# Windowed attention scores: tiles of 64 queries of two heads in place of 128 queries of one head

## The chip, the cores and the metric

The kernel runs on one core of a Trainium2 chip, as one program. Its time is the device time of one execution in microseconds; lower is better. The time before is 1047.88 us, the median of three runs (1046.16 to 1048.37).

## The reference, cut to what matters

One encoder block over T = 1040 positions (16 meta tokens and 1024 positions of the sequence), with D = 1024. From one input projection come a retention branch (4 heads) and an attention branch (8 heads in 2 groups of keys, head dimension 128), each with a SiLU gate and a projection; sigmoid gates merge them, and an output projection, a norm and a residual end the block. The change lies in the attention branch:

```python
ok = (jnp.abs(qpos[:, :, None] - kp) <= WINDOW) & (kp >= CHUNK) & (kp < Lp)   # WINDOW = CHUNK = 128
s_band = jnp.einsum("bnqgrd,bnkgd->bngrqk", qb, kb) * scale
s_band = jnp.where(ok[None, :, None, None], s_band, NEG_INF)
s_meta = jnp.einsum("bnqgrd,bmgd->bngrqm", qb, km) * scale
s = jnp.concatenate([s_band, s_meta], axis=-1)
m = jnp.maximum(jnp.max(s, axis=-1, keepdims=True), sink_l)
p = jnp.exp(s - m)
p = p / (jnp.sum(p, axis=-1, keepdims=True) + jnp.exp(sink_l - m))
o = (jnp.einsum("bngrqk,bnkgd->bnqgrd", p[..., :3 * CHUNK], vb)
     + jnp.einsum("bngrqm,bmgd->bnqgrd", p[..., 3 * CHUNK:], vm))
```

A query sees the keys at most 128 positions away on either side, the 16 meta keys, and a sink logit that adds to the sum alone. A block of 128 queries so sees parts of three blocks of keys: 384 keys, and 16 meta keys.

## The kernel before

Every fp32 matrix product is made of three fp32r products: both operands are split into a rounded high part and the rest, and `mm3` (L74) issues high x high (L76), low x high (L77) and high x low (L78). Splits are a copy on ACT or POOL for the high part and a subtraction on DVE (`dve_lo`, L92) for the low part.

The program is written in the order in which engines are to be fed; a scheduler turns it into a list per engine, and `follow` (L81) ties instructions behind others. The stages are: projections and retention, head by head; then attention, into which projections of later heads and products of the next stage are woven as filling; then gates (z), the two branch projections (r and a) and the output projection (o).

Attention (L1379) runs over `chunks`: four pairs of heads `hp` (two heads `e_` of one group of keys), and for each eight blocks `n` of 128 queries. A chunk passes three stages:

- `stage1` (L1384): six score matmuls into two banks of PSUM, 128 queries of one head by a span of key columns each. The keys of a group lie in `kh` and `kl` with the 16 meta keys repeated in each 272 columns, so one span of 400 columns holds the three blocks and the meta keys (272 columns for block 0 and block 7). One DVE instruction (L1416) adds the mask, scales, keeps the minimum against the negated sink and writes `raw`; ACT takes the exponential with its sum (L1419), the sink's column with it; DVE takes the reciprocal `den` (L1422); POOL scales both heads' weights `p` in place (L1429) and copies the meta columns twice into `pm2` (L1437, recorded as L89). In the last two chunks ACT does POOL's part (L1426, L1435).
- `stage2` (L1440): TensorE transposes the weights, 128 columns at a time: L1446 for two blocks of keys, L1451 for the third, L1452 for the meta columns; ACT and DVE split them.
- `stage3` (L1476): TensorE multiplies with the values (`po`), ACT copies the result to `oa` (L1487), and it goes out by DMA.

In program order a round is: stage1 of chunk k+1, stage2 of chunk k, filling (`fill`, by `FILL`, mostly 5 to 9 steps of three matmuls of 512 columns), stage3 of chunk k-1. The scores of a chunk are so made one round before its weights are transposed. Queries are rotated by `rope_late` (L180, two accumulating DMAs on POOL's queue) and split by `split_q` (L661: ACT L667, DVE L92) per head and half of the sequence; `BEGUN` (L1539) says at which step of the filling.

Of the kernel before, what the change touches and what calls it, by code (L numbers as in the profile page):

```python
# [7 lines left out]
F32 = mybir.dt.float32  # L8
# [31 lines left out]
def block_kernel(ctx: ExitStack, tc: tile.TileContext, x0, xT, x, meta, w_in, w_rb, w_ab, w_out, post_w,  # L40
# [52 lines left out]


    vec = keep.tile([P, 2 * KT], F32, name="vec")
    nsink = edge.tile([P, 24], F32, name="nsink")[:, 0:8]
# [169 lines left out]
    with tc.tile_pool(name="setup", bufs=1, reuse_waits="tile") as st:  # L266
# [81 lines left out]
            qk0_mm(k)  # L348
        decay_columns()
        with follow(low):  # L350
            nc.vector.tensor_scalar(nsink, head[:, 29:37], -1.0, None, op0=ALU.mult)
# [308 lines left out]

    def split_q(hp, e_, i):  # L661

        o = aq[hp][e_, i]
        h, l = (aw.tile([P, 512], R, tag=f"aq{t}", bufs=4, name=f"aq{t}{hp}_{i}{e_}") for t in "hl")
        if not aqs:
            aw.tile([P, 48], F32, name="space_aq")
        nc.scalar.copy(h, o)  # L667
        dve_lo(l, o, h)
        aqs[hp, e_, i] = h, l


    def fetch_aq(hp):
# [703 lines left out]
    for t in pm:  # L1376
        nc.vector.memset(t.bitcast(F32), 0.0)

    def attention():  # L1379
        oa = [None]  # L1380
        raw = [aw.tile([P, 401], F32, tag=f"raw{e_}", bufs=1, name=f"raw{e_}") for e_ in range(2)]
        st1, st2 = {}, {}

        def stage1(hp, n):  # L1384
            g = hp // 2
            kh, kl = (t.rearrange("p a b -> p (a b)") for t in kT[g])
            if n == 0:
                start, wid, mo, blocks, moff = 0, 272, 144, [(0, 0), (1, 128)], 256
            else:
                start = 272 * ((n - 1) // 2) + 128 * ((n - 1) % 2)  # L1390
                mo = 0
                wid = 272 if n == 7 else 400
                if n % 2:
                    blocks, moff = [(n - 1, 0), (n, 128), (n + 1, 272)], 256
                else:
                    blocks, moff = [(n - 1, 0), (n, 144), (n + 1, 272)], 128
                if n == 7:
                    blocks = blocks[:2]
            i, o0 = n // 4, P * (n % 4)
            nm_ = ap.tile([P, 2], F32, tag="nm", bufs=3, name=f"nm{hp}_{n}")  # L1400
            den = ap.tile([P, 2], F32, tag="den", bufs=3, name=f"den{hp}_{n}")
            pt = []
            pp = ap.tile([P, 2, 401], F32, tag="p", bufs=2, name=f"p{hp}_{n}")
            for e_ in range(2):
                hd = 2 * hp + e_
                if (hp, e_, i) not in aqs:
                    split_q(hp, e_, i)
                a_, b_ = (t[:, o0:o0 + P] for t in aqs[hp, e_, i])
                s = p2(f"ps{hd}_{n}")
                mm3(s[:, 0:wid], a_, b_, kh[:, start:start + wid], kl[:, start:start + wid], True, True)  # L1410
                if n == 0:
                    if hp:
                        raw[e_] = aw.tile([P, 401], F32, tag=f"raw{e_}", bufs=1, name=f"raw{hd}")
                    nc.vector.tensor_copy(raw[e_][:, 0:1], nsink[:, hd:hd + 1])
                p = pp[:, e_]
                nc.vector.tensor_tensor_reduce(raw[e_][:, 1:1 + wid], s[:, 0:wid], mask[0][:, mo:mo + wid], -SCALE,  # L1416
                                               nsink[:, hd:hd + 1], ALU.add, ALU.min, nm_[:, e_:e_ + 1])

                last["exp"] = nc.scalar.activation(p[:, 0:1 + wid], raw[e_][:, 0:1 + wid], AF.Exp, scale=-1.0,  # L1419
                                                   bias=nm_[:, e_:e_ + 1], accum_out=den[:, e_:e_ + 1]).ins  # L1420
                pt.append(p[:, 1:401])
            last["sum"] = nc.vector.reciprocal(den, den).ins  # L1422
            softmax.append(last["sum"])
            for e_ in range(2):
                if hp == 3 and n > 5:
                    softmax.append(nc.scalar.activation(pt[e_][:, 0:wid], pt[e_][:, 0:wid], AF.Copy,  # L1426
                                                        scale=den[:, e_:e_ + 1]).ins)
                    continue
                nc.gpsimd.tensor_scalar(pt[e_][:, 0:wid], pt[e_][:, 0:wid], den[:, e_:e_ + 1], 1.0, op0=ALU.mult,  # L1429
                                        op1=ALU.mult)  # L1430
# [3 lines left out]
            if hp == 3 and n > 5:  # L1434
                softmax.append(nc.scalar.copy(both, w_).ins)  # L1435
            else:
                pool_hi(both, w_)  # L1437
            st1[hp, n] = (pt, blocks, both.rearrange("p a b c -> p (a b c)"))

        def stage2(hp, n):  # L1440
            pt, blocks, both = st1.pop((hp, n))
            t1 = p1(f"pt1_{hp}_{n}")
            for j in range(2):
                for e_ in range(2):
                    o = blocks[j][1]
                    nc.tensor.transpose(t1[:, 256 * j + P * e_:256 * j + P * e_ + P], pt[e_][:, o:o + P], ident)  # L1446
            t2 = p1(f"pt2_{hp}_{n}")
            if len(blocks) > 2:
                for e_ in range(2):
                    o = blocks[2][1]  # L1450
                    nc.tensor.transpose(t2[:, 256 + P * e_:256 + P * e_ + P], pt[e_][:, o:o + P], ident)  # L1451
# [24 lines left out]
        def stage3(hp, n):  # L1476
# [121 lines left out]
def _constants():  # L1598
    import numpy as np

    f = np.float32
    half = 64
    inv = (f(10000.0) ** (-np.arange(half, dtype=f) * f(2.0) / f(128.0))).astype(f)
    pos = np.arange(T, dtype=f)
    ang = pos[:, None] * inv[None, :]
    c, s = np.cos(ang).T.astype(f), np.sin(ang).T.astype(f)
    rope = np.stack([np.concatenate([c, c], 0), np.concatenate([s, -s], 0)])
    j = np.arange(P)
    prev = np.where(j[None, :] >= j[:, None], 0.0, -1e30)
    nxt = np.where(j[None, :] <= j[:, None], 0.0, -1e30)  # L1610
    z = np.zeros((P, 144))
    rel = j[None, :] - j[:, None]
    idx = np.stack([127 - j, j, j + 1, 128 - j, np.maximum(15 - j, 0)], 1)
    tab = np.concatenate([prev, z, nxt, z[:, :16], np.eye(P), np.maximum(rel, 0), np.maximum(-rel, 0)], 1)
    return np.ascontiguousarray(rope), np.ascontiguousarray(tab.astype(f)), idx.astype(f)


def arrange(inputs):
# [5 lines left out]
    def units(w, order):  # L1624
# [10 lines left out]
    xT = con(np.concatenate([meta, x], 0).T.reshape(KT, P, T))  # L1635
    dec = np.concatenate([i["ret_decay_fwd"][0], i["ret_decay_bwd"][0]])
    small = [i["pre_norm_w"][0].reshape(KT, P).T, i["ret_norm_w"][0].reshape(KT, P).T, np.tile(dec, (P, 1)), idx,
             np.tile(i["attn_sink"][0], (P, 1)), np.zeros((P, 3), np.float32)]
    nat = list(range(8))
    return {  # L1640
        "x0": con(np.concatenate(small + [xT[0]], 1)),
# [31 lines left out]
```

## Time and profile before

| | |
|---|---|
| median of three runs | 1047.88 us (1046.16 to 1048.37) |
| the profiled execution | 1045.47 us |
| its span, first to last instruction | 1043.4 us |
| granted TensorE clock | 0.998 |
| DVE, ACT, POOL busy | 80%, 48%, 22% of the span |
| attention, about 332 to 546 us | 214 us |

Times of the trace are counted from the span's start. A group's row ends with busy time in all, mean of one, and the idle time of its engine just before it with what ended it. A record of a matmul is as long as its way through the array, and consecutive ones overlap; their starts tell their price. PEld is the loading of a stationary operand, which lies beside other matmuls.

### The profile page before, as it was taken

The numbers are of one execution on the slowest core, as the hardware profiler recorded it, in microseconds if no ns is written. First come the engines' busy times: TensorE is split into PE (matmuls) and PEld (weight loads), VectorE is DVE, ScalarE is ACT, GpSimd is POOL, SyncE is SP. The second block draws the span as 40 slices with busy tenths as digits, with TensorE's granted clock in tenths as the row PEclk, the third lists the DMA queues.
The fourth block names the chain that finished last, engine by engine and source line by source line (L and its number), as shares of the span: only waits on it lengthen the run. The fifth ranks groups of instructions, "written<-read, shape, count | busy, mean of one in ns | idle before, by whom it ended". The sixth has DMA issues, their size and how long they took to land. (4 is left out here: it accounts for less than half of the span.)

```text
span 1043.4 us, 17240 instructions
## 1 busy us (share of the span) xinstructions
PE 1029.0 (99%) x5880; PEld 901.9 (86%) x5880; DVE 838.1 (80%) x1788; ACT 505.7 (48%) x1127; POOL 228.2 (22%) x338
## 2 busy tenths in 40 slices
PE   9999999999999999999999999999999999999997
PEld 8998999989989888988888888777888788788886
DVE  7786758768875787878769988998899899778665
ACT  5541432423524566665677554555557446334443
POOL 3444244243342333443310000000000000111042
PEclk9999999999999999999999999999999999999999
DMA  9434223243231466676549679899935746799563
GB/s 353 165 88 88 64 46 85 78 88 103 78 91 62 102 182 188 172 184 164 162 165 340 191 255 322 308 325 346 392 109 178 248 159 231 223 236 317 134 122 80
DMA packets 98838, 188.43 MB, mean 181 GB/s; under 512 B 13024, under 2 KB 37632, under 8 KB 98192
## 3 DMA queue, kind: packets, MB, share of 16 engines
q1 hardware_dynamic: 81200, 162.89, 46.5%
q0 software_dynamic: 10176, 14.73, 9.4%
q10 hardware_dynamic: 7376, 9.73, 2.7%
q8 instruction: 46, 0.75, 0.3%
q14 instruction: 40, 0.33, 0.1%
HBM read 124.32 MB, written 57.68 MB: 174 GB/s over the span
## 5 line engine op out<-in xcount | busy, mean ns | idle before, releaser
L1287 POOL DMA_DIRECT2D mx_d<-c1a x4 | 3.6, 889 | 395.7 <-DVE c1a L1278 377.5
L77 PE MATMUL bz<-big,llz 128*128 128x512 f32 x192 | 74.9, 390 | 0.2 <-DVE llz L92 0.2
L76 PE MATMUL bz<-big,lhz 128*128 128x512 f32 x192 | 74.0, 390 | 0.5 <-ACT lhz L974 0.5
L78 PE MATMUL bz<-big,lhz 128*128 128x512 f32 x192 | 74.2, 389 | 0.0
L76 PE MATMUL pv<-wh,big 128*128 128x256 f32 x256 | 72.8, 284 | 0.0
L77 PE MATMUL pv<-wh,big 128*128 128x256 f32 x256 | 72.7, 284 | 0.0
L78 PE MATMUL pv<-wl,big 128*128 128x256 f32 x256 | 72.7, 284 | 0.0
L77 PE MATMUL bz<-T,llz 128*128 128x512 f32 x176 | 68.6, 390 | 0.7 <-DVE llz L92 0.7
L76 PE MATMUL bz<-T,lhz 128*128 128x512 f32 x176 | 68.2, 390 | 0.5 <-DVE u2z L1064 0.5
L78 PE MATMUL bz<-T,lhz 128*128 128x512 f32 x176 | 68.5, 389 | 0.0
L1419 ACT ACTIVATE p<-raw,nm 128x401 f32<-128x401 f32 (+1 forms) x64 | 38.3, 600 | 34.7 <-DVE nm L1416 33.3
L1429 POOL TENSOR_SCALAR p<-p,den 128x400 f32<-128x400 f32 (+1 forms) x60 | 37.8, 687 | 67.1 <-DVE den L1422 65.2
L76 PE MATMUL paq<-big,wh 128*128 128x512 f32 x128 | 51.5, 402 | 0.0
L77 PE MATMUL paq<-big,wl 128*128 128x512 f32 x128 | 50.2, 392 | 0.1
L78 PE MATMUL paq<-big,wh 128*128 128x512 f32 x128 | 50.2, 393 | 0.0
L76 PEld LDWEIGHTS pv<-wh,big 128*128 128x128 f32 x256 | 48.3, 189 | 0.4
L77 PEld LDWEIGHTS pv<-wh,big 128*128 128x128 f32 x256 | 48.3, 189 | 0.4
L78 PEld LDWEIGHTS pv<-wl,big 128*128 128x128 f32 x256 | 48.2, 188 | 0.3
L76 PEld LDWEIGHTS bz<-big,lhz 128*128 128x128 f32 x192 | 36.1, 188 | 8.5 <-ACT lhz L974 1.1
L92 DVE TENSOR_TENSOR wl<-wr,wh 128x1024 fp32r<-128x1024 f32 x28 | 35.1, 1258 | 10.0 <-POOL wh L89 6.7
L77 PEld LDWEIGHTS bz<-big,llz 128*128 128x128 f32 x192 | 36.0, 188 | 7.9 <-DVE llz L92 0.5
L78 PEld LDWEIGHTS bz<-big,lhz 128*128 128x128 f32 x192 | 36.0, 188 | 7.5
(616 smaller groups left out, 3594.7 us busy)
## 6 DMA issues: line engine op xcount, KB each, us to landing
wrz<-in_w_in_dram SPq DMA_DIRECT2D x32, 512.0 KB, 6.1
wr<-in_w_in_dram SPq DMA_DIRECT2D x29, 512.0 KB, 4.0
we<-in_w_in_dram SPq DMA_DIRECT2D x16, 512.0 KB, 4.2
tg<-tg_d SPq DMA_DIRECT2D x32, 256.0 KB, 4.9
e<-e ACTq DMA_DIRECT2D x20, 256.0 KB, 2.6
e<-e SPq DMA_DIRECT2D x20, 256.0 KB, 4.9
xn<-in_x_dram SPq DMA_DIRECT2D x8, 512.0 KB, 9.6
oTr_d<-ost SPq DMA_DIRECT2D x16, 256.0 KB, 2.1
```

Source lines behind the costliest of these rows:

```text
L76: nc.tensor.matmul(o, ah, bh, start=first, stop=False, **kw)
L77: nc.tensor.matmul(o, al, bh, start=False, stop=False, **kw)
L78: latest[:] = [nc.tensor.matmul(o, ah, bl, start=False, stop=last, **kw).ins]
L92: return nc.vector.tensor_tensor(o, i, hi.bitcast(F32), ALU.subtract).ins
L1287: nc.gpsimd.dma_start(d, to, accum_op=ALU.add)
L1419: last["exp"] = nc.scalar.activation(p[:, 0:1 + wid], raw[e_][:, 0:1 + wid], AF.Exp, scale=-1.0, bias=nm_[:, e_:e_ + 1], accum_out=den[:, ...
L1429: nc.gpsimd.tensor_scalar(pt[e_][:, 0:wid], pt[e_][:, 0:wid], den[:, e_:e_ + 1], 1.0, op0=ALU.mult, op1=ALU.mult)
```

## The change

A score tile is now 64 queries of both heads of a pair (128 rows: 64 of the first head, 64 of the second), and a chunk has two of them, `x_` = 0 for the first 64 queries and 1 for the last, in place of one tile per head. The first 64 queries of a block never see the last 64 keys of the span, and the last 64 never see the first 64, so each span is 336 columns instead of 400; block 7's second tile has 208, and block 0's tiles keep 272, the second with a mask of its own (`late_mask`). So that transposes can still take 128 columns each, the weights lie in two lasting tiles with 64 columns that are zeroed once: behind the span for the first tile, ahead of it for the second. With that come: queries of both heads in one stationary tile, written with a stride by `split_q`; a sink per row, so `nsink` has one column per pair; the sink's column behind the span in the second tile, which is filled anew for blocks 0 and 7; a meta copy per tile instead of one for both; and an output copy that sorts the columns back. Counts of score matmuls, masks, exponentials, scalings, transposes and value products are the same.

```diff
     def split_q(hp, e_, i):
-        o = aq[hp][e_, i]
-        h, l = (aw.tile([P, 512], R, tag=f"aq{t}", bufs=4, name=f"aq{t}{hp}_{i}{e_}") for t in "hl")
+        o = aq[hp][e_, i].rearrange("p (t q) -> p t q", q=64)
+        if (hp, i) not in aqs:
+            aqs[hp, i] = [aw.tile([P, 1024], R, tag=f"aq{t}", bufs=2, name=f"aq{t}{hp}_{i}") for t in "hl"], set()
...
+        h, l = (t.rearrange("p (t e q) -> p t e q", e=2, q=64)[:, :, e_] for t in aqs[hp, i][0])
         nc.scalar.copy(h, o)
         dve_lo(l, o, h)
...
+    late_mask = aw.tile([P, 320], F32, name="late_mask")[:, 0:272]
+    nc.vector.memset(late_mask, 0.0)
+    nc.vector.tensor_copy(late_mask[:, 192:256], mask[0][:, 272:336])
+    weights = [ap.tile([P, 2, 401], F32, name=f"p{i}") for i in range(2)]
+    for t in weights:
+        nc.vector.memset(t[:, 0, 337:401], 0.0)
+        nc.vector.memset(t[:, 1, 0:64], 0.0)
...
+        def window(n, x_):
+            if n == 0:
+                return 0, 272, (late_mask if x_ else mask[0][:, 144:416]), [(0, 0), (1, 128)], 256
+            start = 272 * ((n - 1) // 2) + 128 * ((n - 1) % 2) + 64 * x_
+            wid = (208 if x_ else 272) if n == 7 else 336
+            own, moff = (128, 256) if n % 2 else (144, 128)
+            blocks = [(n - 1, -64 * x_), (n, own - 64 * x_), (n + 1, 272 - 64 * x_)]
+            return start, wid, mask[0][:, 0:wid], blocks[:2 if n == 7 else 3], moff - 64 * x_
...
-            for e_ in range(2):
-                hd = 2 * hp + e_
-                if (hp, e_, i) not in aqs:
-                    split_q(hp, e_, i)
-                a_, b_ = (t[:, o0:o0 + P] for t in aqs[hp, e_, i])
-                s = p2(f"ps{hd}_{n}")
+            for e_ in range(2):
+                if (hp, i) not in aqs or e_ not in aqs[hp, i][1]:
+                    split_q(hp, e_, i)
+            for x_ in range(2):
+                start, wid, seen, blocks, moff = window(n, x_)
+                a_, b_ = (t[:, P * (2 * (n % 4) + x_):P * (2 * (n % 4) + x_ + 1)] for t in aqs[hp, i][0])
+                s = p2(f"ps{hp}_{n}_{x_}")
                 mm3(s[:, 0:wid], a_, b_, kh[:, start:start + wid], kl[:, start:start + wid], True, True)
...
+                for c in ({0: (272, 336), 7: (208,)} if x_ else {0: (0,)}).get(n, ()):
+                    nc.vector.tensor_copy(r[:, c:c + 1], nsink[:, hp:hp + 1])
+                o, w0 = (0, 64) if x_ else (1, 1)
...
-            w_ = pp[:, :, 1 + moff:1 + moff + NM].unsqueeze(2).to_broadcast([P, 2, 2, NM])
-                pool_hi(both, w_)
+            for x_, (_, w0, _, moff) in enumerate(sides):
+                w_ = pp[:, x_, w0 + moff:w0 + moff + NM].unsqueeze(1).to_broadcast([P, 2, NM])
+                    pool_hi(both[:, x_], w_)
...
-            last["oa"] = nc.scalar.copy(oa[0][:, :, o0:o0 + P],
-                                        po[:, 0:256].rearrange("p (e t) -> p e t", e=2)).ins
+            last["oa"] = nc.scalar.copy(oa[0][:, :, o0:o0 + P].rearrange("p e (x q) -> p e x q", x=2),
+                                        po[:, 0:256].rearrange("p (x e q) -> p e x q", x=2, e=2)).ins
```

More of the change, by code (lines that the diff above doesn't have):

```diff
@@ L95, in block_kernel @@
     vec = keep.tile([P, 2 * KT], F32, name="vec")
-    nsink = edge.tile([P, 24], F32, name="nsink")[:, 0:8]
+    nsink = edge.tile([P, 24], F32, name="nsink")[:, 0:4]
     dtab = keep.tile([P, 28], F32, name="dtab")
@@ L1386, in stage1 @@
             kh, kl = (t.rearrange("p a b -> p (a b)") for t in kT[g])
[L1387 to L1398, printed above, removed]
@@ L1415, in stage1 @@
[L1415 to L1421, printed above, removed]
+                if n == 0 and hp:
+                    raw[x_] = aw.tile([P, 337], F32, tag=f"raw{x_}", bufs=1, name=f"raw{hp}_{x_}")
@@ new lines, in stage1 @@
+                r = raw[x_]
+                for c in ({0: (272, 336), 7: (208,)} if x_ else {0: (0,)}).get(n, ()):
+                    nc.vector.tensor_copy(r[:, c:c + 1], nsink[:, hp:hp + 1])
+                o, w0 = (0, 64) if x_ else (1, 1)
+                nc.vector.tensor_tensor_reduce(r[:, o:o + wid], s[:, 0:wid], seen, -SCALE,
+                                               nsink[:, hp:hp + 1], ALU.add, ALU.min, nm_[:, x_:x_ + 1])
+                last["exp"] = nc.scalar.activation(pp[:, x_, w0 - o:w0 - o + 1 + wid], r[:, 0:1 + wid], AF.Exp,
+                                                   scale=-1.0, bias=nm_[:, x_:x_ + 1],
+                                                   accum_out=den[:, x_:x_ + 1]).ins
@@ L1422, in stage1 @@
+                sides.append((wid, w0, blocks, moff))
             last["sum"] = nc.vector.reciprocal(den, den).ins
             softmax.append(last["sum"])
-            for e_ in range(2):
[L1425 to L1430, printed above, removed]
@@ new lines, in stage1 @@
+            ends = hp == 3 and n > 5
+            for x_, (wid, w0, _, _) in enumerate(sides):
+                v = pp[:, x_, w0:w0 + wid]
+                if ends:
+                    softmax.append(nc.scalar.activation(v, v, AF.Copy, scale=den[:, x_:x_ + 1]).ins)
+                else:
+                    nc.gpsimd.tensor_scalar(v, v, den[:, x_:x_ + 1], 1.0, op0=ALU.mult, op1=ALU.mult)
+            for x_, (_, w0, _, moff) in enumerate(sides):
+                w_ = pp[:, x_, w0 + moff:w0 + moff + NM].unsqueeze(1).to_broadcast([P, 2, NM])
+                if ends:
+                    softmax.append(nc.scalar.copy(both[:, x_], w_).ins)
+                else:
+                    pool_hi(both[:, x_], w_)
@@ L1440, in stage2 @@
+            pt = [lambda o, x_=x_, w0=w0: pp[:, x_, w0 + o:w0 + o + P] for x_, (_, w0, _, _) in enumerate(sides)]
+            st1[hp, n] = (pt, [b for _, _, b, _ in sides], both.rearrange("p a b c -> p (a b c)"))
         def stage2(hp, n):
-            pt, blocks, both = st1.pop((hp, n))
+            pt, sides, both = st1.pop((hp, n))
+            blocks = sides[0]
             t1 = p1(f"pt1_{hp}_{n}")
             for j in range(2):
-                for e_ in range(2):
-                    o = blocks[j][1]
-                    nc.tensor.transpose(t1[:, 256 * j + P * e_:256 * j + P * e_ + P], pt[e_][:, o:o + P], ident)
+                for x_ in range(2):
+                    nc.tensor.transpose(t1[:, 256 * j + P * x_:256 * j + P * x_ + P], pt[x_](sides[x_][j][1]), ident)
@@ L1447, in stage2 @@
             t2 = p1(f"pt2_{hp}_{n}")
             if len(blocks) > 2:
-                for e_ in range(2):
-                    o = blocks[2][1]
-                    nc.tensor.transpose(t2[:, 256 + P * e_:256 + P * e_ + P], pt[e_][:, o:o + P], ident)
+                for x_ in range(2):
+                    nc.tensor.transpose(t2[:, 256 + P * x_:256 + P * x_ + P], pt[x_](sides[x_][2][1]), ident)
             latest[:] = [nc.tensor.transpose(t2[0:4 * NM, 0:P], both, ident).ins]
@@ L1608, in _constants @@
     j = np.arange(P)
-    prev = np.where(j[None, :] >= j[:, None], 0.0, -1e30)
-    nxt = np.where(j[None, :] <= j[:, None], 0.0, -1e30)
-    z = np.zeros((P, 144))
+    k, q = np.arange(half)[None, :], (j % half)[:, None]
+    prev, nxt = (np.where(seen, 0.0, -1e30) for seen in (k >= q, k <= q))
+    z = np.zeros((P, 208))
+    unseen = np.full((P, half), -1e30)
     rel = j[None, :] - j[:, None]
     idx = np.stack([127 - j, j, j + 1, 128 - j, np.maximum(15 - j, 0)], 1)
-    tab = np.concatenate([prev, z, nxt, z[:, :16], np.eye(P), np.maximum(rel, 0), np.maximum(-rel, 0)], 1)
+    tab = np.concatenate([prev, z, nxt, unseen, z[:, :16], np.eye(P), np.maximum(rel, 0), np.maximum(-rel, 0)], 1)
     return np.ascontiguousarray(rope), np.ascontiguousarray(tab.astype(f)), idx.astype(f)
```

26 lines of the change are left out of this document (9 added, 17 removed).

## The prediction

> **What bounds the kernel now.** I read the page's busy table and its slices first, then the attention stage by windows, then the groups of that stage with their shapes kept apart, then the timeline of TensorE for the distance between starts, and last the waits of the stage.
>
> ```profile
> span 1043.4 us, 17240 instructions
> ## 1 busy us (share of the span) xinstructions
> PE 1029.0 (99%) x5880; PEld 901.9 (86%) x5880; DVE 838.1 (80%) x1788; ACT 505.7 (48%) x1127; POOL 228.2 (22%) x338
> ## 2 busy tenths in 40 slices
> PE   9999999999999999999999999999999999999997
> ```
>
> The second line is to be read against the last: TensorE (PE) is busy in every slice, so there is no stage in which another engine sets the pace. Scores and softmax stand between about 332 and 546 us, and there too:
>
> ```profile
> 332.00:546.00 214.00, 212.75 (x1260) 188.65 (x1259) 164.46 (x411) 131.95 (x347) 73.34 (x126) 1.00 0.57 159
> ```
>
> Columns: window, its length, then PE, PEld, DVE, ACT and POOL busy, PEclk, DMA share and GB/s. TensorE works 212.75 of 214 us at the full granted clock; DVE has 50 us free, ACT 82, POOL 141. So what an edit takes from TensorE's own stream shortens the run, and what it takes from or gives to DVE, ACT and POOL counts only where TensorE then waits less or more.
>
> A busy figure doesn't price a matmul, since consecutive ones overlap: the price is the distance between starts. From the timeline of TensorE, three stretches without a wait:
>
> ```profile
> 339.43 0.34 PE L76 MATMUL ps<-kTh,aqh 128*128 128x400 f32 x1
> ...
> 340.52 0.60 PE L1446 MATMUL pt<-ident,p 128*128 128x128 f32 x4
> ```
>
> ```profile
> 434.86 0.29 PE L76 MATMUL ps<-kTh,aqh 128*128 128x272 f32 x1
> ...
> 435.61 0.27 PE L1446 MATMUL pt<-ident,p 128*128 128x128 f32 x1
> ```
>
> ```profile
> 330.71 0.39 PE L76 MATMUL paq<-big,wh 128*128 128x512 f32 x1
> ...
> 332.77 0.42 PE L76 MATMUL ps<-kTh,aqh 128*128 128x272 f32 x2
> ```
>
> Six score matmuls of 400 columns lie between the first two rows: 1.09 us, 0.182 each, though the record says 0.34. Six of 272 columns: 0.75 us, 0.125 each. Nine of 512: 2.06 us, 0.229 each. The first two give a slope of 0.057/128 = 0.445 ns per column; carried on to 512 it gives 0.232, close to the 0.229 seen, so the line is straight here.
>
> **The narrower score matmuls (the gain).** A block of 128 queries and two heads had six matmuls of 400 columns; now it has six of 336 (two tiles of 64 queries by two heads, three products each). Blocks 1 to 6 of four head pairs: 24 x 6 = 144 matmuls. By the line, 336 columns cost 0.125 + 64 x 0.000445 = 0.1535 us, 0.0285 less than 400. 144 x 0.0285 = **-4.1 us**. Both ends of the interpolation are measured on the same operands, so I allow only 0.2 either way. The order of instructions on TensorE is the same in both kernels but for swaps inside single score and transpose groups, so these savings are taken out of the same stream.
>
> **The one shape that is new.** Block 7's second tile has 208 columns instead of 272: 4 x 3 = 12 matmuls. All fp32r matmuls of the trace stream 256 columns or more, so this must be bounded. Cheapest: the line, 0.097 us. Next, the distance between transposes of 128 columns, each of which also loads a 128-column operand:
>
> ```profile
> 349.85 0.60 PE L1446 MATMUL pt<-ident,p 128*128 128x128 f32 x4
> 350.29 0.38 PE L1451 MATMUL pt<-ident,p 128*128 128x128 f32 x2
> ```
>
> 0.44 us for four is 0.11 each, nearly twice the 0.061 that the line gives for 128 columns, so a start comes no sooner than about 0.11 us after the one before. Dearest: the plain fp32 products of the retention part, one call in the code and two records here:
>
> ```profile
> 46.69 0.39 PE L490 MATMUL tr<-qr,kr 128*128 128x128 f32 x2
> ...
> 47.03 0.28 PE L77 MATMUL pv<-wh,big 128*128 128x256 f32 x1
> ```
>
> Between these starts lie that call and one matmul of 256 columns (0.118 by the line): 0.34 - 0.118 = 0.22 us for 128 columns, so 0.36 us for 208 if a narrow fp32r product fell to that rate. Range for the twelve: 12 x (0.097 - 0.125) = -0.3 to 12 x (0.36 - 0.125) = +2.8 us. I take 0.11, **-0.2 us**, as the next operand's load is what the neighbouring row shows at small widths, and the fp32r type did nothing odd between 272 and 512. The dear end is a rival below. The Trainium skill, "FP8 and Floating Point Precision", section "TensorE Precision Notes", says that a true FP32 product takes four passes through the array and the reduced-precision form reads the same words truncated; an estimate from it is 4 x 208 columns on the line, 0.37 us, +2.9 us in all. The two records of 0.22 us agree with four passes; no run here shows that width decides it.
>
> **The work before the first scores.** DVE gets a memset and a copy for the late mask, four memsets of 64 zero columns and more sink copies ahead of the query splits. Before:
>
> ```profile
> 328.72 0.55 DVE L1377 MEMSET pm<- 128x256 f32 x2
> ...
> 331.42 0.48 DVE L905 SCALAR_TENSOR_TENSOR val<-pav,rcol,vah 128x256 fp32r<-128x256 f32 x1 [2.14 <-ACT vah L904]
> 331.82 0.14 DVE L1414 COPY raw<-nsink 128x1 f32<-128x1 f32 x1
> 331.93 1.29 DVE L92 TENSOR_TENSOR aql<-aq,aqh 128x512 fp32r<-128x512 f32 x2
> ```
>
> ```profile
> 333.02 0.29 PE L77 MATMUL ps<-kTh,aql 128*128 128x272 f32 x1
> ```
>
> The new order of DVE puts the late mask's memset with those of pm (DVE idles for 2.14 us before 331.42, so it costs nothing), but the four small memsets, two more sink copies and the mask copy between 331.8 and the end of the second split. And both heads now share one stationary tile, so the first score product with a low half waits for both splits, not one. Seven small instructions of about 0.1 us (a copy of one column is 0.14 with its latency, a memset of 256 columns 0.27) put the second split's end at 333.22 + 0.7 = 333.9, and the matmul of 333.02 starts about 333.95: **+0.9 us**, once. Bounds: 0.2 (both splits waited for, nothing else) and 1.6 (every memset at 0.27). Behind it three projection matmuls, the next scores and twelve more stand on TensorE before the first transpose, so nothing more is lost. For later heads the splits end before their scores start, and the order keeps that.
>
> **The softmax chain.** The groups of the stage, shapes apart:
>
> ```profile
> L1429 POOL TENSOR_SCALAR p<-p,den 128x400 f32<-128x400 f32 x46 | 29.0, 670 | 49.8 <-DVE den L1422 47.9 <-PE pe L78 1.9
> L1416 DVE CUSTOM_DVE_ANT_0 raw<-ps,mask,nsink 128x400 f32<-128x400 f32 x48 | 28.8, 631 | 3.7 <-PE ps L78 3.6
> ...
> L1429 POOL TENSOR_SCALAR p<-p,den 128x272 f32<-128x272 f32 x14 | 8.8, 744 | 17.3 <-DVE den L1422 17.3
> L89 POOL TENSOR_SCALAR pm<-p 128x64 f32<-128x64 f32 x30 | 8.6, 288 | 2.5
> ...
> L1416 DVE CUSTOM_DVE_ANT_0 raw<-ps,mask,nsink 128x272 f32<-128x272 f32 x16 | 7.5, 496 | 2.2 <-PE ps L78 2.2
> ```
>
> Masking goes from 631 to 496 + 64 x (135/128) = 564 ns, two in a row: -0.13 us per block. The scaling on POOL is not cheaper by the narrow row (744 against 670), because some of its runs met a busy DVE; I take nothing to -0.2 us per block. The meta copy becomes two, at most 0.29 us more on POOL. The chain per block so moves by -0.3 to +0.2 us. Where that counts:
>
> ```profile
> PEld pt L1446 <- POOL p L1429: 2.2, 6, 0.5
> ```
>
> ```profile
> 467.87 0.27 PE L1451 MATMUL pt<-ident,p 128*128 128x128 f32 x1
> 468.42 0.55 PE L1446 MATMUL pt<-ident,p 128*128 128x128 f32 x3 [0.28 <-POOL p L1429]
> ```
>
> ```profile
> 466.44 1.93 POOL L1429 TENSOR_SCALAR p<-p,den 128x400 f32<-128x400 f32 x2
> ```
>
> The transposes wait for POOL in six cases only; here the scaling ends at 468.37 and the transposes start behind it. Two ordinary blocks look like this:
>
> ```profile
> 337.61 1.19 POOL L1429 TENSOR_SCALAR p<-p,den 128x400 f32<-128x400 f32 x2 [0.86 <-DVE den L1422]
> ...
> 344.66 0.25 POOL L89 TENSOR_SCALAR pm<-p 128x64 f32<-128x64 f32 x1
> ```
>
> POOL is done at 344.91 and the transposes of that block start at 349.85 (shown above): 4.9 us of projection matmuls cover it. The block before it had its scaling done at 338.80 and its transposes at 340.52, 1.7 us later. So about five blocks of 32 gain or lose what the chain moves: 5 x -0.3 to 5 x +0.2. I take **-0.5 us**, for the masking is the surest part, with -1.3 and +1.0 as ends. The output copy and the split copies only change their strides; DVE and ACT have the free time above, and I cost them nothing.
>
> **The sum.** -4.1 - 0.2 + 0.9 - 0.5 = **-3.9 us**. The profiled execution took 1045.47 us (2.1 around its span), which would become 1041.6; the median of the three runs shown is 1047.88, 2.4 higher, and becomes **1044.0 us**.
>
> **Rivals.**
>
> *Narrow products are slow* (the 208-column shape at the plain fp32 rate): -4.1 + 2.8 + 0.9 - 0.5 = -0.9, 1047.0 us. For it: no narrow fp32r product in the whole trace, and a rate of that kind exists on this array. Against it: the row of 0.11. It is within 0.2% (2.1 us) of before, about what a measurement of this kernel can tell from no change.
>
> *The gain is given back at the next late transfer*: the stage ends 4 us sooner, and what comes behind it waits for its weights. That gives 0, 1047.9 us. Against it: those transfers are issued in the same order behind the same instructions, so they come sooner too.
>
> *POOL becomes the late one* (slower). Four POOL instructions per block stand where three did, and the narrow scaling row is dearer than the wide one. If the chain grew by 1.5 us per block, the blocks with the least cover (twelve of 32 have less than 2.5 us) would begin to wait; with this cover, from the end of the scaling to the first transpose, read for all 32 blocks as for the three above (none, 1.7 us, 5.3 us), the shortfalls add up to 8.5 us, so 8.5 - 4.1 - 0.2 + 0.9 = +5.1, 1053.0 us. It decides from a growth of about 1.0 us per block on (shortfalls of 5.5 us, +2.1 in all). Against it: two meta copies at 0.288 would have to turn into more than 1.2 us. The Trainium skill, "GPSIMD Engine Reference", section "8. Key points", says that GpSimd shares its SBUF interfaces with VectorE and suffers from instructions with two SBUF inputs; the 1.93 us for two scalings at 466.44, against 2 x 0.67 on the mean, is in line with that.
>
> **How the numbers follow.** Forecast 0.66, narrow products 0.19, gain given back 0.08, POOL late 0.07. The forecast's terms alone reach from 1047.88 - 4.3 - 0.3 + 0.2 - 1.3 = 1042.2 to 1047.88 - 3.9 - 0.2 + 1.6 + 1.0 = 1046.4; the three runs differ by 2.2 us, so I go to 1041.6 below, and above to the narrow case with some of that spread, 1047.6. Faster by over 0.2% means below 1045.8: nearly all of the forecast and a little of the narrow case, 0.66. The same: most of the narrow case, the given-back case and the forecast's upper end, 0.26. Slower: 0.08.
>
> **What the profile after would show.** The score groups at 336 columns with starts 0.153 us apart and at 208 with 0.11 (0.36 if the rival holds); the first low product of the stage near 333.95; waits of the transposes for POOL of 2.2 us or less; the stage 332 to 546 about 4 us shorter and everything behind it shifted by the same. I am wrong if starts at 336 are more than 0.16 apart, if the 208 shape shows two records for one call, if transposes wait for POOL in more than ten blocks, or if the stretch behind 546 grows.

## The result, and the profile after

| | before | after |
|---|---|---|
| median (runs) | 1046.89 us (10) | 1043.06 us (10) |
| ratio, 95% interval | | 0.9963 (0.995 to 0.9976), -3.9 us |
| the same kernels, a second set of runs | 1045.4 us (23) | 1043.36 us (11) |
| ratio, 95% interval | | 0.9975 (0.9966 to 0.9983), -2.6 us |
| the profiled executions | 1045.47, second set 1047.34 | 1044.06, second set 1043.36 |

By the ratios the change makes the kernel 2.6 to 3.9 us faster (the medians of the second set lie 2.0 us apart); 1044.0 had been predicted. The first pair of profiled executions differs by 1.4 us only, so the profiles have to be read by stages, and twice (the second profiles come from the experiments e7 and e8). One part of the gain lies in no stage: the device time is 2.10 to 2.12 us longer than the span on the mean in every set of runs of a kernel with the tiles of before, and 1.76 to 1.79 in every one with the new tiles. These 0.3 us were not predicted, and nothing here shows what they are.

The page after, busy table, and the attention stage by windows (window, length, PE, PEld, DVE, ACT, POOL busy, granted clock, DMA share, GB/s):

```profile
span 1042.3 us, 17315 instructions
...
PE 1025.3 (98%) x5880; PEld 898.8 (86%) x5880; DVE 834.9 (80%) x1802; ACT 502.5 (48%) x1129; POOL 227.9 (22%) x368
...
332.00:546.00 214.00, 212.05 (x1277) 187.83 (x1276) 162.00 (x428) 130.35 (x353) 74.23 (x156) 1.00 0.59 165
```

TensorE still works through the whole stage at the full clock. As many matmuls as before lie on it, and their distances are to be read from its timeline after; the first two rows are the ends of a group of six scores, the others a tile of block 7:

```profile
335.65 0.32 PE L76 MATMUL ps<-kTh,aqh 128*128 128x336 f32 x1
...
336.42 0.32 PE L78 MATMUL ps<-kTl,aqh 128*128 128x336 f32 x1
...
435.01 0.25 PE L76 MATMUL ps<-kTh,aqh 128*128 128x208 f32 x1
435.10 0.28 PE L77 MATMUL ps<-kTh,aql 128*128 128x208 f32 x1
435.21 0.28 PE L78 MATMUL ps<-kTl,aqh 128*128 128x208 f32 x1
435.32 0.60 PE L1458 MATMUL pt<-ident,p 128*128 128x128 f32 x4
```

Five distances of 336 columns take 0.77 us, 0.154 each; three of 208 take 0.31 us, 0.103 each, one record per call. The start of the stage, DVE and then TensorE:

```profile
332.06 0.48 DVE L907 SCALAR_TENSOR_TENSOR val<-pav,rcol,vah 128x256 fp32r<-128x256 f32 x1 [1.86 <-ACT vah L906]
332.51 0.11 DVE L1386 MEMSET p<- 128x64 f32 x1
...
332.83 0.68 DVE L92 TENSOR_TENSOR aql<-aq,aqh 128x512 fp32r<-128x512 f32 x1
...
333.59 0.69 DVE L92 TENSOR_TENSOR aql<-aq,aqh 128x512 fp32r<-128x512 f32 x1
```

```profile
333.41 0.41 PE L76 MATMUL ps<-kTh,aqh 128*128 128x272 f32 x2
334.33 0.40 PE L77 MATMUL ps<-kTh,aql 128*128 128x272 f32 x1 [0.51 <-DVE aql L92]
```

The first product with a low half starts 0.92 us behind the first score, where it was 0.25: it waits for the second split, as foretold. The whole stage begins 0.64 us later than in the first profile of before, but that lies in front of the change: the setup ahead of the first retention products (`pv`) took 28.4 to 30.6 us from one execution to another, and everything from there to the first score 303.06 in both kernels.

The groups of the stage after (busy, mean ns of one | idle before), and TensorE's waits for other engines:

```profile
L1442 POOL TENSOR_SCALAR p<-p,den 128x336 f32<-128x336 f32 x46 | 26.0, 590 | 48.4 <-DVE den L1433 45.8 <-PE pe L78 1.3 <-PE pak L78 1.2
L1426 DVE CUSTOM_DVE_ANT_0 raw<-ps,mask,nsink 128x336 f32<-128x336 f32 x48 | 25.4, 564 | 3.4 <-PE ps L78 3.2
...
L89 POOL TENSOR_SCALAR pm<-p 128x32 f32<-128x32 f32 x60 | 14.8, 288 | 0.0
...
L1442 POOL TENSOR_SCALAR p<-p,den 128x208 f32<-128x208 f32 x3 | 3.3, 1116 | 0.0
```

```profile
PEld pt L1458 <- POOL p L1442: 1.4, 3, 0.7
...
PEld ps L77 <- DVE aql L92: 1.1, 2, 0.7
...
PEld pt L1463 <- POOL pm L89: 0.7, 2, 0.5
```

The masking takes 564 ns, exactly the figure worked out, and the scaling 590 instead of 670; yet the transposes wait for POOL no less than before (1.4 + 0.7 here, 2.7 + 0.7 in the second profile, 2.2 + 0.3 in the first of before). "2.2 us or less" had been foretold.

To separate what the matmuls cost from what they wait, I split the distances between starts in the stage, first score to last: the median distance behind each shape, taken over the whole trace and summed up over the stage, is the stream; what goes beyond it is put down as a wait to the operation that starts late.

| us | stage | stream | waits ahead of scores | ahead of transposes | other |
|---|---|---|---|---|---|
| before, two profiles | 207.90 / 208.44 | 200.83 / 200.83 | 0.10 / 0.11 | 2.89 / 3.41 | 4.08 / 4.10 |
| after, two profiles | 204.50 / 205.54 | 196.67 / 196.67 | 0.97 / 0.61 | 2.91 / 4.31 | 3.95 / 3.95 |

The stream is the same to 0.01 us in two executions of a kernel, and 4.16 us shorter after. It is made of medians in whole nanoseconds, so its size hangs on how they are taken: with the medians of the stage alone it is 202.24 and 201.77 before, 197.61 and 197.62 after, 4.2 to 4.6 us less. The waits vary by 0.5 and 1.0 us between executions of the same kernel, and they grew by about 1 us.

The waits ahead of the transposes lie in few rounds:

| us | before, two profiles | after, two profiles | e12 (below) |
|---|---|---|---|
| four rounds with a late scaling: block 7 of the first pair of heads, 4 of the second, 3 and 7 of the third | 1.65 / 1.58 | 2.13 / 2.52 | 0.01 |
| block 2 of the third pair, 458 to 462 us | 1.12 / 1.70 | 0.52 / 1.53 | 1.33 |
| all others | 0.12 / 0.13 | 0.26 / 0.26 | 0.26 |

In the round of block 2 TensorE waits for DVE's split of weights that were transposed a round earlier. There the executions of one kernel differ most; these are its transposes in the two profiles of before:

```profile
460.18 0.88 PE L1446 MATMUL pt<-ident,p 128*128 128x128 f32 x4 [0.24 <-DVE pal L92]
```

```profile
460.72 0.88 PE L1446 MATMUL pt<-ident,p 128*128 128x128 f32 x4 [0.81 <-DVE pal L92]
```

So the spread has a place, and the four late rounds can be compared without it: they wait 0.5 to 0.9 us more after.

### The profile page after: what moved, and what is told of

Its sections match the earlier page's. It is cut to its first block, busy times and chain, and to the rows that moved or that the text cites. A ratio compares the mean times of both kernels' runs of the same rounds, so it can differ in the third digit from the quotient of the medians.

```text
span 1042.3 us, 17315 instructions
## 1 busy us (share of the span) xinstructions
PE 1025.3 (98%) x5880; PEld 898.8 (86%) x5880; DVE 834.9 (80%) x1802; ACT 502.5 (48%) x1129; POOL 227.9 (22%) x368
## 5 line engine op out<-in xcount | busy, mean ns | idle before, releaser
L1429 ACT ACTIVATE p<-raw,nm 128x337 f32<-128x337 f32 (+1 forms) x64 | 35.5, 556 | 33.1 <-DVE nm L1426 31.6
L1442 POOL TENSOR_SCALAR p<-p,den 128x336 f32<-128x336 f32 (+2 forms) x60 | 34.6, 624 | 66.7 <-DVE den L1433 64.1
```

What stands on the lines that cost most here:

```text
L1429: last["exp"] = nc.scalar.activation(pp[:, x_, w0 - o:w0 - o + 1 + wid], r[:, 0:1 + wid], AF.Exp, scale=-1.0, bias=nm_[:, x_:x_ + 1], accu ...
L1442: nc.gpsimd.tensor_scalar(v, v, den[:, x_:x_ + 1], 1.0, op0=ALU.mult, op1=ALU.mult)
```

## The experiments

Each ratio is to runs of before on the same chip, with its 95% interval.

**Wide scores again in the new tiles (e1, and the same kernel again as e10).** All six products at 400 columns (272 in blocks 0 and 7), the softmax as narrow as after:

```diff
-                mm3(s[:, 0:wid], a_, b_, kh[:, start:start + wid], kl[:, start:start + wid], True, True)
+                lead = 64 * x_ if n else 0
+                wide = 272 if n in (0, 7) else 400
+                mm3(s[:, 0:wide], a_, b_, kh[:, start - lead:start - lead + wide],
+                    kl[:, start - lead:start - lead + wide], True, True)
+                s = s[:, lead:lead + wid]
```

> The changed kernel, but its score matmuls stream 400 columns again (272 in blocks 0 and 7); mask, exponential and scaling still take 336. Theory (the gain is TensorE's columns): 144 x 0.0285 + 0.2 = 4.3 us come back, about 1047.4 us, ratio to the kernel before 1.000, starts of the scores 0.182 apart. Rival (the gain is the shorter softmax chain, through fewer waits): it stays where the changed kernel is, about 1043.1 us, ratio 0.996.

> The kernel e1_wide_scores (two-head tiles with every score product 400 columns wide again) unchanged, as a second sample: its first time ratio was 0.9985 where its stage, 207.93, is that of before. If the narrow softmax is worth nothing, the ratio is 0.9993 to 1.001 this time and the stage 207.5 to 208.8; if 0.9985 was right, it comes again, and some stage is shorter than in both profiles of before.

Measured: 0.9985 (0.9976 to 0.9994), and again 0.9993 (0.9983 to 1.0003). The stream is 200.83 both times, that of before: the 4.16 us of the stream are the columns. The stage is 207.93 and 207.06, since the transposes wait less than in any profile of before or after, 2.31 and 1.40 us. So the 0.7 to 1.6 us that remain to before have a place: the stages are 0.7 us shorter on the mean, and 0.3 us lie outside the span, as in every kernel with the new tiles. POOL's timeline shows what is behind it: block 7 of the third pair, in before, after and here.

```profile
493.30 1.68 POOL L187 DMA_DIRECT2D aq<-m_aq  x2 [6.58 <-ACT pbh L1467]
494.42 2.26 POOL L1429 TENSOR_SCALAR p<-p,den 128x272 f32<-128x272 f32 x2
```

```profile
491.60 1.68 POOL L187 DMA_DIRECT2D aq<-m_aq  x2 [7.11 <-ACT pah L1468]
492.73 2.19 POOL L1442 TENSOR_SCALAR p<-p,den 128x272 f32<-128x272 f32 x2
494.18 1.52 POOL L89 TENSOR_SCALAR pm<-p 128x32 f32<-128x32 f32 x2
```

```profile
493.34 0.92 POOL L1446 TENSOR_SCALAR p<-p,den 128x272 f32<-128x272 f32 x2 [6.58 <-DVE den L1437]
494.23 0.22 POOL L89 TENSOR_SCALAR pm<-p 128x32 f32<-128x32 f32 x1
494.41 1.68 POOL L187 DMA_DIRECT2D aq<-m_aq  x2
```

The row's "x2" in the second fence holds one scaling of 272 and one of 208 columns. In before and after POOL first issues the two DMAs of a rotation; the scaling starts 1.13 us later and runs more than twice as long, and the transposes are late. Here the scheduler put the rotation behind the scaling, which takes 0.92 us, and the transposes have 2.5 us to spare. This happened in block 7 of the third pair only; in the other three late rounds the rotation stays ahead, and they wait 1.09 and 1.04 us in all. It is an order on POOL, then, more than the narrower softmax; the experiment e12 tests that.

**Columns alone (e5, again as e11).** The kernel before, its tiles and softmax unchanged, with two of the three products of blocks 1 to 6 at 336 columns:

```diff
+                cut = 336 if wid == 400 else wid
+                nc.tensor.matmul(s[:, 0:wid], a_, kh[:, start:start + wid], start=True, stop=False)
+                nc.tensor.matmul(s[:, 0:cut], b_, kh[:, start:start + cut], start=False, stop=False)
+                latest[:] = [nc.tensor.matmul(s[:, 0:cut], a_, kl[:, start:start + cut], start=False, stop=True).ins]
```

> The kernel before, with one thing changed: the two low score products of blocks 1 to 6 stream 336 columns, so the low parts of the last 64 keys are left out. Layout, mask, exponential, POOL are as before. Theory (columns): 96 x 0.0285 = 2.7 us less, ratio 0.9974. Rival (the chain): nothing changes, ratio 1.000.

> The kernel e5_columns_alone (before with the two low products at 336 columns in blocks 1 to 6, and the low parts of the last 64 keys left out) unchanged, as a second sample: its first ratio was 0.9959 and its stage 204.37, where 96 matmuls by 0.028 us make 2.7 us or 0.9974. If the column count alone is the cause, the ratio comes back at 0.997 to 0.9975 and the stage at 205 to 205.7, the rest having been spread of the waits; if shorter products also bring the chain forward, the 0.9959 and 204.4 come again.

Measured: 0.9959 (0.9947 to 0.9972), and again 0.9966 (0.9953 to 0.9979). The stream is 198.19 in both, 2.64 us less than before: 96 x 0.0275. The stage came to 204.37 and 205.38, the difference being the waits of the transposes, 2.19 and 3.20: 0.44 and 1.45 of them stand in the round at 458 us, and the four late rounds wait 1.53 and 1.52, as before. The second stage lies where the column count puts it, and the first 1.0 us below by the spread of that one round. The run times gained 3.6 and 4.3 us, more than the 2.6 of the stream; 2.6 lies inside the second interval and just outside the first, and what the rest is stays open.

**POOL made late (e3).** The kernel after, with a further pass of POOL over the weights, `pool_hi(v, v)` behind each scaling.

> The changed kernel with each scaling on POOL followed by a second pass over the same weights, times one: the chain grows by two passes of 0.54, 1.08 us per block. Theory (cover read from the trace of the changed kernel, end of the scaling to the first transpose, shortfalls added up over 32 blocks): 5.3 us more, about 1048.4 us, ratio to the kernel before 1.0015, and transposes wait for POOL in about ten blocks. Rival (POOL lies beside TensorE and costs nothing): 1043.1 us, 0.996. Rival (a growth costs every block): 32 x 1.08 = 35 us.

Measured: 1.0019 (1.001 to 1.0028). The waits of the trace:

```profile
PEld pt L1459 <- POOL p L89: 6.0, 9, 1.8
...
PE pt L1459 <- POOL p L89: 4.0, 4, 1.6
```

Stream 196.74, waits ahead of transposes 8.26: all of the loss is there. The cover read for the rival "POOL becomes the late one" was priced right, 5.3 us expected and 4.5 to 5.5 measured in the stage (210.01), and the change is far from it: in an ordinary block the two meta copies cost 0.40 us together.

**POOL made early (e6).** The kernel after, scaling only the first tile on POOL (`elif x_ == 0:` in place of `else:`); it leaves the weights of the second tile undivided.

> The kernel after, with the scaling of the second tile's weights on POOL left out in every block where POOL did it (so those weights stay undivided): the chain in front of the transposes is 0.59 us shorter per block. Theory (only the four or five blocks without cover feel the chain): each gains at most what it waits now, 1.7 us in the listed waits of 0.23, 0.40, 0.66 and 0.39 us; the attention stage 1.2 to 2.0 us shorter than the 204.5 of after, all other blocks unchanged, ratio near 0.995. Rival (the chain is off the path altogether and those waits come from another engine): no change, ratio 0.9963, waits of the transposes still 2.8 us in sum.

Measured: 0.9953 (0.9941 to 0.9966); stage 203.55, waits ahead of transposes 2.07. They are shorter than the 2.91 and 4.31 of after and don't go away: 1.36 us of what is left belong to one round, at 457 to 459 us, about half of it for a split on DVE. That is the round with the spread. The four late rounds fall from 2.13 and 2.52 us to 0.39 with the rotation still ahead of them, so there the chain counts as much as expected.

**Start of the stage mended (e2).** The kernel after, with the memsets and the late mask's copy on POOL and one meta copy for both tiles.

```diff
-    nc.vector.memset(late_mask, 0.0)
-    nc.vector.tensor_copy(late_mask[:, 192:256], mask[0][:, 272:336])
+    nc.gpsimd.memset(late_mask, 0.0)
+    pool_hi(late_mask[:, 192:256], mask[0][:, 272:336])
...
-        nc.vector.memset(t[:, 0, 337:401], 0.0)
-        nc.vector.memset(t[:, 1, 0:64], 0.0)
+        nc.gpsimd.memset(t[:, 0, 337:401], 0.0)
+        nc.gpsimd.memset(t[:, 1, 0:64], 0.0)
...
```

> The changed kernel with the late mask and the zero columns made on POOL, which is idle then, and one meta copy for both tiles in place of two. Theory: the wait of 0.67 us before the first low score product falls to 0.3 or less, the waits for the meta copy (0.7) go, together 0.5 to 1.1 us less than the changed kernel, about 1042.3 us, ratio to the kernel before 0.9955. Rival: DVE was behind anyway, no change, 0.9963.

Measured: 0.9963 (0.9949 to 0.9977). The first low product waits 0.26 us instead of 0.67, so the small DVE instructions do make that wait, but 0.4 us can't be seen in the time. The stage is 204.31 us. With one meta copy the four late rounds wait 1.60 us, as much as before; in this one profile the waits that the change added there are gone, so the second copy has a part in them, of unknown size.

**Second samples of both kernels (e7, e8).**

> The kernel before, unchanged, as a second sample of it: ratio 1.000 within 0.0015, and its profile a second reading of the stage between the first and last scores (207.9 us before). If the waits of the transposes in that stage (2.9 us in sum) come back within 0.3 us, then the 0.7 us by which they are shorter in the kernel that narrows columns alone is an effect of it; if they differ by 0.5 us or more, it is the spread from one execution to the next.

> The kernel after, unchanged, as a second sample of it: ratio 0.9963 within 0.0015, and the stage between the first and last scores 204.5 us within 0.5. The wait of the first low score product 0.67 us again, since nothing but the order of DVE sets it; the waits of the transposes 2.9 us in sum if they are an effect of the code, anything between 2.2 and 3.5 if they are spread. The 1.6 us by which its final-projection stage was longer than that of before should not come back.

Measured: before against itself 1.0003 (0.9993 to 1.0014), after 0.9975 (0.9966 to 0.9983). The waits of the transposes came at 3.41 and 4.31 us, so 0.5 to 1.4 us of them is spread, 0.6 and 1.0 of it in the round at 458 us. The wait at the start came again, 0.67. The stretch from the first gate product to the first branch product, 246.49 and 248.18 in the first pair of profiles, was 247.93 and 246.94 in the second, and 246.06 to 248.54 over the profiles of all versions: the 1.7 us that seemed to be lost there after are spread too.

**The price of a width (e4).** Groups of 30 matmuls of one width; rows of the timeline of TensorE, start of a group first:

> The whole block computation is left out. The kernel holds groups of 30 reduced-precision matmuls (fp32r) on two alternating 128x128 operands, at 512, 400, 336, 272, 256, 240, 208, 192, 160, 128, 96 and 64 columns, then plain fp32 groups of 256, 208 and 128 columns. Theory (the distance between starts is a straight line in the columns until the next operand's load sets it, and a width under 256 does not change the rate): starts 0.227 us apart at 512, 0.182 at 400, 0.154 at 336, 0.125 at 272, 0.117 at 256, then a floor near 0.11 for every width from 240 down, one record per call; plain fp32 two records per call and about 0.36 us a call at 208 and 0.22 at 128. Rival (narrow products are slow): from the first width under 256 the fp32r groups stand at the plain fp32 distance, 0.36 us at 208, with two records per call.

```profile
21.04 6.96 PE L33 MATMUL narrow__131<-hi,wt 128*128 128x512 f32 x30
27.84 5.57 PE L33 MATMUL narrow__163<-hi,wt 128*128 128x400 f32 x30
33.24 4.76 PE L33 MATMUL narrow__195<-hi,wt 128*128 128x336 f32 x30
37.84 3.92 PE L33 MATMUL narrow__227<-hi,wt 128*128 128x272 f32 x30
...
45.19 3.52 PE L33 MATMUL narrow__291<-hi,wt 128*128 128x240 f32 x30
48.55 3.50 PE L33 MATMUL narrow__323<-hi,wt 128*128 128x208 f32 x30
51.89 3.50 PE L33 MATMUL narrow__355<-hi,wt 128*128 128x192 f32 x30
...
84.95 10.71 PE L33 MATMUL plain__547<-raw 128*128 128x208 f32 x60
95.50 6.86 PE L33 MATMUL plain__579<-raw 128*128 128x128 f32 x60
```

From start to start of groups: 6.80 us at 512, 5.40 at 400, 4.60 at 336, that is 0.227, 0.180 and 0.153 each. At 240 and at 208 it is 3.36 and 3.34, 0.112 and 0.111, and no less down to 96 columns: the floor. Every group alternates two operands, so no run shows whether loading the next one is what sets it. The plain fp32 groups have two records per call; 208 columns take 10.55 us, 0.352 a call, and at 128 0.22. The dear rate exists and belongs to the type, not to the width.

**The second scaling on ACT (e9).** The kernel e2, with

```diff
+                elif x_:
+                    nc.scalar.activation(v, v, AF.Copy, scale=den[:, x_:x_ + 1])
```

> The kernel e2_mended with the scaling of the second tile's weights moved from POOL to ACT, so that the two scalings of a block run beside each other; nothing is left out. Theory (the blocks without cover wait for the chain, and a chain 0.5 us shorter shortens their waits, as leaving that scaling out did: attention stage 203.55 against 204.5 and 205.5): stage 203.2 to 204.0, ratio near 0.995, waits of the transposes for POOL under 1 us. Rival (ACT is in order: a scaling that waits there for the reciprocal of DVE holds up the copies of the attention outputs and the splits queued behind it, and new waits for ACT take the place of those for POOL): stage 204.3 or longer, ratio 0.997 or above.

Measured: 1.0001 (0.9992 to 1.0009), stage 208.30: the numbers of the rival. ACT and TensorE at the worst place:

```profile
457.39 1.05 ACT L118 CAST wh<-wr 128x1024 fp32r<-128x1024 f32 x1
458.34 1.33 ACT L754 ACTIVATE xs<-xs,vec 128x512 f32<-128x512 f32 x2
459.57 0.57 ACT L1442 ACTIVATE p<-p,den 128x336 f32<-128x336 f32 x1
```

```profile
457.56 0.30 PE L1461 MATMUL pt<-ident,p 128*128 128x128 f32 x1 [1.39 <-DVE pal L92]
458.70 0.45 PE L1465 MATMUL pt<-ident,p 128*128 128x128 f32 x1 [0.84 <-DVE pbl L92]
460.19 0.90 PE L1461 MATMUL pt<-ident,p 128*128 128x128 f32 x3 [1.05 <-ACT p L1442]
```

The last of these waits is not for what is queued behind the scaling, as I had put it, but for the scaling itself: it stands behind 2.2 us of other ACT work, and the transposes behind it. The two waits ahead of it belong to the splits that are late in this round in nearly every version: the round waits 4.43 us here and 1.69 in e2. In the four late rounds the theory held, 0.34 us in place of 1.60.

**The rotation behind the scaling (e12).** The kernel after, with

```diff
+    scaled = []
...
-        for r in (0, 64):
-            nc.gpsimd.dma_start(o[64 - r:128 - r, 0:n], m[r:r + 64, 0:n], accum_op=ALU.add)
+        with follow(*scaled):
+            for r in (0, 64):
+                nc.gpsimd.dma_start(o[64 - r:128 - r, 0:n], m[r:r + 64, 0:n], accum_op=ALU.add)
...
-                    pool_hi(both[:, x_], w_)
+                    scaled[:] = [pool_hi(both[:, x_], w_)]
```

> The kernel after, with the DMA issues of the query and key rotation on POOL's queue tied behind the weights' scaling and meta copies that stand before them in the program; nothing is left out. This moves them in five rounds only, among them the four whose transposes wait for POOL (blocks 7 of the first and third pair, block 4 of the second, block 3 of the third). Theory (those blocks are late because 1.1 us of DMA issue stands ahead of their scaling, and not because a chain of ordinary length is too long): the waits between the transposes and ahead of them fall from 2.9 and 4.3 us in the two profiles of after to 1 to 2 us, the attention stage from 204.5 and 205.5 to 203 to 204, ratio 0.994 to 0.996. Rival (the rotated queries and keys now come later, and their splits and the scores that need them wait instead): stage 204.5 or longer, with new waits of score or key products for the splits, ratio 0.9965 or above.

Measured: 0.9954 (0.9936 to 0.9971), 1040.74 against 1045.57 us. POOL at the block shown above, and what the view of waits still puts down to the scaling in the whole stage:

```profile
490.42 0.92 POOL L1445 TENSOR_SCALAR p<-p,den 128x272 f32<-128x272 f32 x2 [6.91 <-DVE den L1436]
491.30 0.40 POOL L89 TENSOR_SCALAR pm<-p 128x32 f32<-128x32 f32 x2
491.88 1.68 POOL L190 DMA_DIRECT2D aq<-m_aq  x2 [0.18 <-issue]
```

```profile
PEld pt L1461 <- POOL p L1445: 0.7, 1, 0.7
```

Stage 203.01, the shortest of all; stream 196.67 as after, waits ahead of transposes 1.60. The row above is the round at 458 us, where the splits are late as well; the four late rounds wait 0.01 us in place of 2.13 and 2.52. So the order on POOL makes these waits, though a shorter chain under the same order takes most of them too (e6). By the stage and by the ratio it is the fastest of the versions that leave nothing out; its interval overlaps those of after, so how much it gains on after rests on the trace (1.5 and 2.5 us of the stage), not on the times.

## Why the prediction was right, and which of its terms were off

- **Narrower scores, -4.1, and the new shape, -0.2.** Together -4.3 predicted, -4.16 measured in the stream. 336 columns have a median of 0.154 us (0.1535 predicted). The 208 shape averages 0.106, between the line's 0.097 and the 0.11 taken; the sweep puts the floor at 0.111. "Narrow products are slow" falls: one record per call in the kernel, 0.111 against 0.352 in the sweep. The Trainium skill, "FP8 and Floating Point Precision", section "TensorE Precision Notes", names four passes for a true fp32 product, 0.37 us by estimate; 0.352 agrees within 6%, and the sweep shows now what no run had then, that the width doesn't bring it on.
- **Start of attention, +0.9.** +0.67 measured, twice; the small DVE instructions follow each other by about 0.07 us, 0.10 at most, and were a little overpriced. "For later heads the splits end before their scores start" failed once, by 0.24 us at 357.9 us of the first profile.
- **Softmax chain, -0.5.** The step that failed. The ordinary chain, first score to end of scaling, did shorten, from 4.44 to 4.01 us in block 2 of the second pair, in both profiles of each. But "about five blocks of 32 gain or lose what the chain moves" took the late blocks to be ordinary ones with little cover. They are not: four of them have the rotation's DMA issues ahead of their scaling, a delay of 1.1 us that the mask's width doesn't touch. In place of the -0.5 they waited 0.5 to 0.9 us more, inside the bound of +1.0 but of the other sign, and with the rotation moved (e12) nothing. In block 7 of the third pair the scaling misses the transposes by 0.71 and 0.78 us after, against 0.43 and 0.36 before; why by more stays open, but for the part of the second meta copy (e2). I had read from the rows for 466 to 468 us only that POOL was late, without asking what it did before.
- **The sum**, -3.9 predicted; the stage shows -3.4 and -2.9, the times -3.9 and -2.6. The 0.3 us outside the span had no term. The first sample's median lies 0.9 us from the 1044.0, which stood on three runs of before at 1047.88; ten give 1046.89. That the ratio gives exactly the predicted -3.9 is luck of the samples to half a microsecond or more. Part of the agreement is errors of opposite sign: the start (0.2 us) and the time outside the span (0.3) came out better than forecast, the chain about 1.2 us worse.
- **"Given back at the next late transfer"**: not seen; from the first gate product to the first branch product the second pair of profiles has 1.0 us less after, the first 1.7 us more. So one sign of being wrong, a longer stretch behind 546, came up in the first pair and not in the second.
- **"POOL becomes the late one"**: not here; e3 shows that it would have cost what was read from the cover.

## What to carry to other kernels

Price a narrower matmul by the distance between starts, interpolated on the same operands, down to a floor (0.111 us here); that term was right to 0.15 us of 4. Before a term for a chain is written down, list the places where it is late and read what each engine on it did just before: if a queue's order causes the lateness, moving one instruction may cure it where a narrower mask didn't. Split a stage into stream and waits, the waits by rounds, and profile each kernel twice, before a difference of 1 us is explained: here most of the spread sat in one round.

## What the runs showed of the hardware that was not expected

A scaling on POOL costs by its place more than by its width: 0.92 us for two of a narrow block alone (e12), 2.19 us right behind two rotation issues and beside a two-input product of DVE (after). That product took 0.98 us there and 0.68 in e12, where the rotation's issues alone ran beside it; so it looks as if scaling and product slow each other, but no run separates them. A narrow group's mean, such as 1116 ns at 208 columns, was that, not the shape: in e12 it is 444.

In e9 the granted clock fell to half. TensorE by windows (window, length, busy of PE, PEld, DVE, ACT, POOL, then the clock):

```profile
456.00:457.00 1.00, 0.18 (x2) 0.00 (x0) 0.44 (x2) 0.99 (x5) 0.73 (x2) 1.00 0.97 229
...
461.30:464.90 3.60, 3.60 (x12) 2.98 (x11) 3.30 (x10) 2.46 (x9) 1.65 (x3) 0.50 0.65 209
```

After some 2 us with little but one transpose on TensorE, from 456.2 on, the clock was 0.75 in the window from 458.0 to 458.5, then 0.50 until about 464.9; starts of 512 columns there are 0.427 us apart. So waits of 4 us cost another 2 us, by an estimate from the starts. In e4 it fell to 0.53 in the microsecond from 68 on, although TensorE was fed without a gap: behind 3 us of matmuls of 64 columns, for about 6 us.

```profile
68.00:69.00 1.00, 1.00 (x7) 1.00 (x7) 0.00 (x0) 0.00 (x0) 0.00 (x0) 0.53 0.00 0
```

The Trainium skill, "TensorE: Matmul & The Clock Gate", Part 1, describes a gate that lets half of the pulses through when TensorE was too idle in windows of 3.4 us. The half rate agrees. In e9 2 us with little work were enough, and in e4 it fell with no idle time in the records; how much work keeps the full clock no run here shows.
